# Order and tile offset of the weight parts in a split-float matmul stream: gate, value, q and k units of an encoder block

## The chip, the cores and the metric

The kernel runs on one core of one Trainium2 chip. The metric is the device time of one execution in microseconds, given as the median of several runs. TensorE (PE) does the matrix products, ScalarE (ACT) and VectorE (DVE) do the elementwise work, GpSimd (POOL) and SyncE (SP) issue most of the DMAs. PEld is the loading of stationary weights into PE, which runs beside its matmuls.

## The reference, cut to what matters

The layer is a bidirectional encoder block on 256 tokens of width 2048, all in float32:

```
h = rmsnorm(x);  [q | k | v | u] = h @ w_in
a = rmsnorm(windowed attention with 12 q heads, 4 kv heads)
f = rmsnorm(Fourier mix of u)
x = x + concat(a, f) @ w_out
h = rmsnorm(x);  up = h @ w_up          # w_up: 2048 x 2*5504
gate, value = up[:, :5504], up[:, 5504:]
act = gelu(depthwise_conv3(gate) + b) * value
y = rmsnorm(x + act @ w_down)
```

The products that matter here are the q and k columns of `h @ w_in` (12 + 4 blocks of 128 columns) and the whole of `h @ w_up` (43 blocks of 128 gate columns and 43 of 128 value columns). Each block contracts over 2048 input features.

## The kernel before, in words

**Split floats.** A float32 operand is kept as two parts that PE reads in a faster format (float32r): a high part, which ACT writes as a rounded copy (L168), and a low part, which DVE writes as the remainder (L169). A product is the sum of high times high, high times low and low times high.

**Units.** The work is a sequence of units, each of which has one weight block of 1 MB (128 partitions x 2048 columns) that SP loads into one of three `raw` tiles. `split` (L161) turns it into a `hi` and a `lo` tile; three buffers of each rotate. Each of these tiles has 2176 columns, and `parts_of` (L154) uses 2048 of them, beginning at an offset in columns that the list `shifts` holds for each unit: a pair, one offset for `hi` and one for `lo`. One column is 4 bytes. One buffer lies 2176 columns, 8704 bytes, behind the other.

**The units of the change** are those of q, k, gate and value. In them the weights are the stationary operand. The 2048 columns of `hi` (and of `lo`) are sixteen slices of 128, one for each 128 input features. `still_weights` (L308) adds up, in one bank of PSUM, for each slice one matmul with the high weights that moves 512 columns (256 tokens' high activations and 256 tokens' low ones, L318), and one with the low weights that moves the 256 high ones (L321). So a unit has 16 matmuls of 512 columns and 16 of 256, and each of the 32 loads its own weights. After it, ACT copies one half of the bank and DVE adds the other (`scaled_sum`), for a q or k unit in `qk_out`.

The argument `group` says how many high matmuls stand ahead of as many low ones. With 1 they alternate; with 16 all sixteen high ones come first. The argument `o` says onto which half of the bank the low product is added. Before, these are:

- q and k: group 1; offsets 16 for `hi`, 0 for `lo`.
- gate j: by j modulo 5 group 1, group 1 with the other half, 2, 4 and 16; offsets 16 and 0.
- value j: group 16; the same offset for both tiles, `16 * (j % 8) + 8 * (j // 32)`: 0, 16, 32 ... 112 for j below 32, then 8, 24 ... 120, and 8, 24, 40 for the last three.
- the first gate and the first value unit are a pair: twelve slices of each, then the last four of each, with group 1. Between them come the transposes of the last quarter of the input.

The units of `w_out` and of the late rows of `w_down` have offset 0 in both tiles; those of u and v have 16 in both. There the weights move and the activations stand.

**Order.** It is written out by hand (`ff_items`, L69): sixteen gate and value units in a row; then four groups, each of three gate or value units in a row and after that thirteen times one product of the down-projection and one unit, and one product. A product (`by_parts`, L1046, tiles `ps_P` and `ps_N`) is twelve matmuls of 512 columns. Behind the groups come four late down units, six gate and value units, and the end. While PE works on an item, the split of the item after the next one is made (`ff_step`).

Of the kernel before, what the change touches and what calls it, by code (L numbers as in the profile page):

```python
# [13 lines left out]
P = 128  # L14
D = 2048
S = 256
NK = D // P
# [12 lines left out]
WARM = 7  # L30

U_HEAD, U_ROW = 16, 768


SHIFT = 16

# [32 lines left out]
def ff_items():  # L69


    def ups(tiles):
        return [(kind, j) for j in tiles for kind in ("gate", "val")]

    items = ups(range(8))
    for g in range(N_GROUPS):
        todo = {
            "u": ups(range(8 * g + 8, 8 * g + 16)),
            "s": [("product", g, c, p) for c in range(2) for p in PRODUCTS[c]],
        }  # L80
        items += [todo[c].pop(0) for c in PATTERN]
        assert not any(todo.values())
    items += [("down", 0, c) for c in range(4)] + ups(LAST)
    items += [("down", 1, c) for c in range(4)] + [("last", c) for c in range(4)]
    return items
# [3 lines left out]
def block_kernel(  # L89
# [18 lines left out]
    nc = tc.nc  # L108
# [10 lines left out]
    def bank(pool, name):  # L119
        return pool.tile([P, 512], F32, tag=pool.name, name=name)  # L120
# [1 line left out]

    units = [(w_u_x[i], 2048) for i in range(4)] + [(w_in[i], 2048) for i in range(20)]
    units += [(w_out[i], 2048) for i in range(16)]
    shifts = [(SHIFT, SHIFT)] * 8 + [(SHIFT, 0)] * 16 + [(0, 0)] * 16
    n_front = len(units)
    items, up_index = ff_items(), {}
    for n, it in enumerate(items):
        if it[0] == "product":
            continue  # L130
        up_index[n] = len(units)
        if it[0] in ("gate", "val"):
            units.append((w_up[2 * it[1] + (it[0] == "val")], 2048))
            if it[0] == "gate":
                shifts.append((SHIFT, 0))
            else:
                j = it[1]
                shifts.append((16 * (j % 8) + 8 * (j // 32),) * 2)
            continue
        elif it[0] == "down":  # L140
            units.append((w_down_late[4 * it[1] + it[2]], 2048))
        else:
            units.append((w_down_last[it[1]], 512 * len(LAST)))
        shifts.append((0, 0))
    RAW = 3
    raws, halves = {}, {}
# [7 lines left out]
    def parts_of(i):  # L154
        halves[i] = tuple(
            wp.tile([P, 2176], F32R, tag=h, name=f"{h}{i}", bufs=3)[:, s : s + 2048]
            for h, s in zip(("hi", "lo"), shifts[i])
        )
        return halves[i]
# [87 lines left out]
    ps = bank(dn, "ps_warm")  # L247
# [57 lines left out]
                ps, ah, wl, start=False, stop=last and q == q0 + len(kk) - 1  # L305
            )

    def still_weights(hi, lo, ps, kk, group=1, o=0):  # L308

        for k0 in kk[::group]:
            ks = range(k0, min(k0 + group, kk[-1] + 1))
            for k in ks:
                s = slice(k * P, (k + 1) * P)
                nc.tensor.matmul(ps, hi[:, s], hk(k), start=k == 0, stop=False)  # L318
            for k in ks:
                s = slice(k * P, (k + 1) * P)  # L320
                nc.tensor.matmul(  # L321
                    ps[:, o : o + S], lo[:, s], hk(k)[:, 0:S], start=False, stop=k == NK - 1
                )

    def hk(k):
        return hT[k // 4][:, k % 4, :]
# [18 lines left out]
    def at(when, i, f, *a):  # L345
        when.setdefault(i, []).append((f, a))
# [17 lines left out]
    for k in range(NK):  # L364
        c, q = k // 4, k % 4
        if q == 0:
            hi, lo = (t.rearrange("p (k c) -> p k c", k=4) for t in parts_of(c))
        n = 1 if c < 2 else 2
# [8 lines left out]
        if k < 4:  # L377

            for p, w in enumerate([hi, hi, lo]):
                for b in range(2):  # L380
                    o = p % 2 * S + b * P
                    nc.tensor.matmul(
                        ps_u[b], hk(k)[:, o : o + P], w[:, q, :],
                        start=k == 0 and p == 0, stop=False,
# [348 lines left out]
    for n, (kind, h) in enumerate(QK_ORDER):  # L733

        def work(hi, lo):
            ps = st["ps", kind, h] = bank(mm, f"ps_{kind}{h}")
            still_weights(hi, lo, ps, range(NK))

        unit(N_QK + n, work)
# [50 lines left out]
    for n, (c, kq) in enumerate(OUT_ORDER):  # L790
# [15 lines left out]
        if kq >= 2:  # L806
            part = "a" if kq == 2 else "f"
            ps = ps_a[c] if kq < 3 else ps_a[c, "f"]
# [113 lines left out]
    def ring_load():  # L922
        if ring_next[0] < len(ring):
            key = ring[ring_next[0]]
            ring_next[0] += 1
            ring_tiles[key] = fp.tile([P, 2048], F32, tag="rawd", name="rawd%d%d%s" % key)
            nc.sync.dma_start(ring_tiles[key], weights_of(*key))
# [24 lines left out]
    def first_sums(g, c):  # L952

        a, b = ring_tiles[g, c, "a"], ring_tiles[g, c, "b"]
        x = ring_tiles["x"] = fp.tile([P, 2048], F32, tag="sumw", name=f"sumw{g}{c}", bufs=1)
        nc.vector.tensor_tensor(x, a, b, ALU.add)
        nc.gpsimd.dma_start(b, weights_of(g, c, "d"), accum_op=ALU.add)
# [14 lines left out]
    def ff_step(n):  # L972
        todo, later[:] = list(later), []
        for f in todo:
            next(f, None)
        run(beside, n)
        split_item(n + 2)
        for f in todo:
            for _ in f:
                pass  # L980
        run(behind, n)

    def up_posts(n, kind, j, ps):
        if kind == "gate":
            at(beside, n + 1, scaled_sum, ps, f"g{j}")
            at(beside, n + 2, gate_conv, j)
            at(behind, n + 2, gate_gelu, j)
        else:
            at(beside, n + 1, scaled_sum, ps, f"v{j}")
            at(beside, n + 2, val_mult, j)  # L990
            if j % 8 == 7 and j < 8 * N_GROUPS:
                g = j // 8
                at(behind, n + 1, operand, g, "P1")
                at(behind, n + 2, operand, g, "N4")
                at(behind, n + 3, operand_sums, g, 0)
                at(behind, n + 4, operand, g, "P7")
                at(behind, n + 4, operand, g, "P2")
                at(behind, n + 5, operand_sums, g, 1)
                at(behind, n + 5, operand, g, "N5")
                at(behind, n + 6, operand, g, "N3")  # L1000
                at(behind, n + 7, operand, g, "P6")
            if j >= 8 * N_GROUPS:
                at(behind, n + 2, act_parts, j)
# [42 lines left out]
    def by_parts(ps, o, hi, lo, first, last):  # L1046

        for p in range(4):
            s = slice(p * 512, (p + 1) * 512)
            nc.tensor.matmul(ps, o[:, 0, p, :], hi[:, s], start=first and p == 0, stop=False)  # L1050
            nc.tensor.matmul(ps, o[:, 1, p, :], hi[:, s], start=False, stop=False)  # L1051
            nc.tensor.matmul(ps, o[:, 0, p, :], lo[:, s], start=False, stop=last and p == 3)  # L1052
# [59 lines left out]
    for q in range(2):  # L1112
        kind, j = items[q]
        ps = bank(mm, f"ps_{kind}{j}")
# [6 lines left out]
    for ps, hi, lo in pair:  # L1121
        still_weights(hi, lo, ps, range(12, NK))
# [7 lines left out]
    for n, it in enumerate(items):  # L1130
        if n < 2:
            continue
        if it[0] == "last":
            break
        if n in (8, 9):
            ring_load()
        if n == 13:
            pending.append(lambda: first_sums(0, 0))
        if it[0] in ("gate", "val"):
            kind, j = it  # L1140
            ps = bank(mm, f"ps_{kind}{j}")
            group, o = ((1, 0), (1, S), (2, 0), (4, 0), (16, 0))[j % 5] if kind == "gate" else (16, 0)
            still_weights(*halves.pop(up_index[n]), ps, range(NK), group, o)
            ff_step(n)
            up_posts(n, kind, j, ps)
            continue
        if it[0] == "product":
            kind, g, c, p = it
            end = g == N_GROUPS - 1
            if (c, p) in held:  # L1150
                by_parts(held[c, p], parts[p], *halves.pop(it), g == 0, end)
            else:
                ps = bank(mm, f"ps_{p}{g}{c}")
                by_parts(ps, parts[p], *halves.pop(it), True, True)
                at(beside, n + 1, product_out, g, c, p, ps)
            if end and p == "N4":
                for q in range(3):
                    at(behind, n + 1 + q, shared_out, c, q)
        else:
            kind, g, c = it  # L1160
            hi, lo = halves.pop(up_index[n])
            ps = [bank(mm, f"ps_l{g}{c}{b}") for b in range(2)]
            for b in range(2):
                moving_weights(hi, lo, 512, LATE[g], act.get, b, ps[b], True, True)
            at(beside, n + 1, down_out, c, ps)
            if (g, c) == (0, 0):
                gfb = fp.tile([P, D], F32, tag="sumw", name="gfb", bufs=1)
                nc.gpsimd.dma_start(gfb, normf_g.partition_broadcast(P))
        ff_step(n)
# [153 lines left out]
```

## Time and profile before

| | |
|---|---|
| median of 3 runs | 964.35 us (964.25 to 964.61) |
| the profiled execution | 965.02 us |
| its span | 963.2 us |
| PE busy | 953.3 us, 99% of the span |
| DVE busy | 751.1 us, 78% |
| ACT busy | 534.3 us, 55% |
| granted TensorE clock | 0.998 |
| DMA over the span | 220 GB/s |

The profile names a group of instructions by line, engine and operation, and by the tiles that it writes and reads. The timeline gives each matmul's start and, in the second column, the time from the start of the first of a merged row to the end of its last. Matmuls overlap: a matmul of 512 columns is shown as some 0.39 us long, while the next one starts some 0.23 us behind it. So the time of a unit is read here from the start of its first matmul to the start of the first matmul of what follows it, and the time of one matmul in a run as that difference over their number (its pitch).

### The profile page before, as it was taken

Reading aid. Unit: us, or ns where it says so; the run is one execution under the profiler, and the core shown is the slowest. Engines: PE = TensorE matmul, PEld = TensorE weight load, DVE = VectorE, ACT = ScalarE, POOL = GpSimd, SP = SyncE. Lnnn points to the kernel's source line nnn. Section 1 sums busy time; section 2 is a strip of 40 time slices with the busy share of each in tenths; the row PEclk is TensorE's granted clock in tenths of the full one; section 3 lists DMA queues with packets and bytes.
Section 4 is the critical chain, followed back from the end, with each engine's and each line's share of the span. In section 5 each row is a group of like instructions: output and inputs, shape, how many; then the busy total and the mean of one; then the engine's idle time right before and its main releaser. Section 6 shows DMA issues by size and latency. Waiting matters only on the chain.

```text
span 963.2 us, 12781 instructions
## 1 busy us (share of the span) xinstructions
PE 953.3 (99%) x5085; PEld 819.9 (85%) x5085; DVE 751.1 (78%) x935; ACT 534.3 (55%) x646; POOL 43.4 (5%) x58
## 2 busy tenths in 40 slices
PE   9999999999999999999999999999999999999996
PEld 7888898888888888888888888888888888888885
DVE  7658877576576788787897978988779979887775
ACT  6656666554454446555665555655556655554442
POOL 0000000000000000000000000000000000000003
PEclk9999999999999999999999999999999999999999
DMA  9854444445546676977778786886977687666532
GB/s 369 319 185 150 157 147 159 150 163 212 181 174 242 234 223 193 289 230 254 229 250 243 238 299 218 262 258 207 287 250 240 200 291 217 214 238 219 176 132 88
DMA packets 32108, 211.58 MB, mean 220 GB/s; under 512 B 3504, under 2 KB 4016, under 8 KB 7984
## 3 DMA queue, kind: packets, MB, share of 16 engines
q1 hardware_dynamic: 28448, 184.55, 51.9%
q0 software_dynamic: 3600, 26.22, 14.2%
q8 instruction: 40, 0.66, 0.3%
q14 instruction: 20, 0.16, 0.0%
HBM read 208.65 MB, written 2.10 MB: 219 GB/s over the span
## 4 chain that ended last, share of the span: by engine, by line
PE 98%; DVE 1%; DMA 0%; issue 0%; ACT 0%; POOL 0%; POOLq 0%; DVEq 0%; ACTq 0%
PE ps_val L318 17%; PE ps_gate L318 17%; PE ps_val L321 8%; PE ps_gate L321 8%; PE ps_q L318 5%; PE ps_P L1052 3%; PE ps_P L1051 3%; PE ps_P L1050 3%; PE ps_q L321 2%; PE ps_N L1052 2%; PE ps_N L1050 2%; PE ps_N L1051 2%; PE ps_a L304 2%; PE ps_a L302 2%; PE ps_a L303 2%; PE ps_k L318 2%
## 5 line engine op out<-in xcount | busy, mean ns | idle before, releaser
L169 DVE TENSOR_TENSOR lo<-raw,hi 128x2048 fp32r<-128x2048 f32 (+1 forms) x133 | 302.7, 2276 | 55.2 <-ACT hi L168 55.2
L168 ACT ACTIVATE hi<-raw 128x2048 fp32r<-128x2048 f32 (+1 forms) x133 | 253.4, 1905 | 60.7 <-PE ps_l L303 25.0
L318 PE MATMUL ps_gate<-hU,hi 128*128 128x512 f32 x688 | 212.2, 394 | 0.0
L318 PE MATMUL ps_val<-hU,hi 128*128 128x512 f32 x688 | 168.4, 394 | 0.0
L318 PEld LDWEIGHTS ps_val<-hU,hi 128*128 128x128 f32 x688 | 128.3, 188 | 29.0
L321 PE MATMUL ps_gate<-hU,lo 128*128 128x256 f32 x688 | 145.7, 280 | 0.0
L318 PEld LDWEIGHTS ps_gate<-hU,hi 128*128 128x128 f32 x688 | 122.5, 188 | 21.4
L321 PEld LDWEIGHTS ps_gate<-hU,lo 128*128 128x128 f32 x688 | 117.2, 188 | 10.0
L321 PEld LDWEIGHTS ps_val<-hU,lo 128*128 128x128 f32 x688 | 88.0, 189 | 3.7
L321 PE MATMUL ps_val<-hU,lo 128*128 128x256 f32 x688 | 90.4, 280 | 0.0
L832 ACT ACTIVATE ft_g<-ps_gate 128x256 f32<-128x256 f32 x43 | 16.6, 385 | 127.6 <-PE ps_gate L321 127.6
L832 ACT ACTIVATE ft_v<-ps_val 128x256 f32<-128x256 f32 x43 | 16.5, 384 | 96.9 <-PE ps_val L321 96.9
L318 PE MATMUL ps_q<-hT,hi 128*128 128x512 f32 x192 | 68.1, 398 | 0.0
L321 PE MATMUL ps_q<-hT,lo 128*128 128x256 f32 x192 | 53.6, 279 | 0.0
L1050 PE MATMUL ps_P<-hi_P,op_P 128*128 128x512 f32 x128 | 50.0, 391 | 0.0
L1052 PE MATMUL ps_P<-lo_P,op_P 128*128 128x512 f32 x128 | 50.0, 391 | 0.0
L1051 PE MATMUL ps_P<-hi_P,op_P 128*128 128x512 f32 x128 | 50.0, 391 | 0.0
L942 DVE TENSOR_TENSOR lo_N<-sumw,hi_N 128x2048 fp32r<-128x2048 f32 x16 | 36.6, 2290 | 10.1 <-ACT hi_N L941 10.1
L318 PEld LDWEIGHTS ps_q<-hT,hi 128*128 128x128 f32 x192 | 36.1, 188 | 8.0
L834 DVE TENSOR_TENSOR fa_g<-ps_gate,ft_g 128x256 f32<-128x256 f32 x43 | 18.2, 423 | 28.8 <-ACT ft_g L832 28.8
L302 PE MATMUL ps_a<-hi,cat 128*128 128x512 f32 x96 | 37.9, 394 | 0.0
L1052 PE MATMUL ps_N<-lo_N,op_N 128*128 128x512 f32 x96 | 37.6, 392 | 0.0
(332 smaller groups left out, 1609.1 us busy)
## 6 DMA issues: line engine op xcount, KB each, us to landing
raw<-in_w_up SPq DMA_DIRECT2D x86, 1024.0 KB, 4.9
raw<-in_w_in SPq DMA_DIRECT2D x20, 1024.0 KB, 4.9
raw<-in_w_out SPq DMA_DIRECT2D x16, 1024.0 KB, 4.8
sumw<-in_w_down POOLq DMA_DIRECT2D x16, 1024.0 KB, 8.6
raw<-in_w_down_late SPq DMA_DIRECT2D x8, 1024.0 KB, 4.7
raw<-in_w_down_last SPq DMA_DIRECT2D x4, 768.0 KB, 4.2
ux<-in_w_u_x SPq DMA_DIRECT2D x3, 768.0 KB, 9.7
xs<-in_x SPq DMA_DIRECT2D x4, 512.0 KB, 16.5
```

What stands on the lines that cost most here:

```text
L168: nc.scalar.activation(hi[:, 0:n], raw[:, 0:n], AF.Copy)
L169: nc.vector.tensor_tensor(lo[:, 0:n], raw[:, 0:n], f32(hi[:, 0:n]), ALU.subtract)
L302: nc.tensor.matmul(ps, ah, wh, start=first and q == q0, stop=False)
L303: nc.tensor.matmul(ps, al, wh, start=False, stop=False)
L304: nc.tensor.matmul(ps, ah, wl, start=False, stop=last and q == q0 + len(kk) - 1)
L318: nc.tensor.matmul(ps, hi[:, s], hk(k), start=k == 0, stop=False)
L321: nc.tensor.matmul(ps[:, o : o + S], lo[:, s], hk(k)[:, 0:S], start=False, stop=k == NK - 1)
L832: nc.scalar.activation(tmp, ps[:, S : 2 * S], AF.Copy)
L942: nc.vector.tensor_tensor(lo, src, f32(hi), ALU.subtract)
L1050: nc.tensor.matmul(ps, o[:, 0, p, :], hi[:, s], start=first and p == 0, stop=False)
L1051: nc.tensor.matmul(ps, o[:, 1, p, :], hi[:, s], start=False, stop=False)
L1052: nc.tensor.matmul(ps, o[:, 0, p, :], lo[:, s], start=False, stop=last and p == 3)
```

## The change

All q, k, gate and value units get one form: sixteen matmuls with the high weights, then sixteen with the low ones, with the low product on the first half of the bank, and both weight tiles without an offset. The pair at the beginning of the up-projection gets twelve and twelve, then four and four. The number of matmuls, what they multiply, the order of the units and the instruction lists of the other engines stay as they are.

```diff
-    shifts = [(SHIFT, SHIFT)] * 8 + [(SHIFT, 0)] * 16 + [(0, 0)] * 16
+    shifts = [(SHIFT, SHIFT)] * 8 + [(0, 0)] * 32
...
             units.append((w_up[2 * it[1] + (it[0] == "val")], 2048))
-            if it[0] == "gate":
-                shifts.append((SHIFT, 0))
-            else:
-                j = it[1]
-                shifts.append((16 * (j % 8) + 8 * (j // 32),) * 2)
+            shifts.append((0, 0))
...
-    def still_weights(hi, lo, ps, kk, group=1, o=0):
-        for k0 in kk[::group]:
-            ks = range(k0, min(k0 + group, kk[-1] + 1))
-            for k in ks:
-                s = slice(k * P, (k + 1) * P)
-                nc.tensor.matmul(ps, hi[:, s], hk(k), start=k == 0, stop=False)
-            for k in ks:
-                s = slice(k * P, (k + 1) * P)
-                nc.tensor.matmul(
-                    ps[:, o : o + S], lo[:, s], hk(k)[:, 0:S], start=False, stop=k == NK - 1
-                )
+    def still_weights(hi, lo, ps, kk):
+        for k in kk:
+            s = slice(k * P, (k + 1) * P)
+            nc.tensor.matmul(ps, hi[:, s], hk(k), start=k == 0, stop=False)
+        for k in kk:
+            s = slice(k * P, (k + 1) * P)
+            nc.tensor.matmul(
+                ps[:, 0:S], lo[:, s], hk(k)[:, 0:S], start=False, stop=k == NK - 1
+            )
...
-            group, o = ((1, 0), (1, S), (2, 0), (4, 0), (16, 0))[j % 5] if kind == "gate" else (16, 0)
-            still_weights(*halves.pop(up_index[n]), ps, range(NK), group, o)
+            still_weights(*halves.pop(up_index[n]), ps, range(NK))
```

## The prediction

> **What bounds the kernel now.** I read the page's busy times and chain first, then the busy times of the middle of the span, then PE's timeline unit by unit.
>
> ```profile
> PE 953.3 (99%) x5085; PEld 819.9 (85%) x5085; DVE 751.1 (78%) x935; ACT 534.3 (55%) x646; POOL 43.4 (5%) x58
> PE 98%; DVE 1%; DMA 0%; issue 0%; ACT 0%; POOL 0%; POOLq 0%; DVEq 0%; ACTq 0%
> L318 PE MATMUL ps_gate<-hU,hi 128*128 128x512 f32 x688 | 212.2, 394 | 0.0
> L321 PE MATMUL ps_val<-hU,lo 128*128 128x256 f32 x688 | 90.4, 280 | 0.0
> ```
>
> PE is the whole chain, and its groups show no idle time ahead of them (the last column). A nanosecond less per matmul is a nanosecond less of the kernel, as long as PE stays supplied. The densest stretch says how far the next engine is:
>
> ```profile
> core 0: us, PE busy (x) PEld busy (x) DVE busy (x) ACT busy (x) POOL busy (x), PEclk, DMA share, GB/s
> 360.00:870.00 510.00, 510.00 (x2704) 437.45 (x2703) 431.64 (x449) 291.89 (x284) 20.69 (x24) 1.00 0.77 243
> ```
>
> DVE has 78 us of 510 free there, against the 5 us or so that PE can lose in it.
>
> The timeline then prices the change, because the value units already have the new order, with many offsets. These are, in order, value 8 (offset 0), value 14 (offset 96), value 16 (0), value 20 (64), gate 24 (16 for high, 0 for low, new order) and value 24 (0):
>
> ```profile
> 355.15 3.84 PE L318 MATMUL ps_val<-hU,hi 128*128 128x512 f32 x16
> 358.83 2.05 PE L321 MATMUL ps_val<-hU,lo 128*128 128x256 f32 x16
> 360.71 3.83 PE L318 MATMUL ps_gate<-hU,hi 128*128 128x512 f32 x16
> ...
> 452.31 3.90 PE L318 MATMUL ps_val<-hU,hi 128*128 128x512 f32 x16
> 456.05 2.05 PE L321 MATMUL ps_val<-hU,lo 128*128 128x256 f32 x16
> 457.94 0.40 PE L1050 MATMUL ps_P<-hi_P,op_P 128*128 128x512 f32 x1
> ...
> 482.97 3.84 PE L318 MATMUL ps_val<-hU,hi 128*128 128x512 f32 x16
> 486.65 1.98 PE L321 MATMUL ps_val<-hU,lo 128*128 128x256 f32 x16
> 488.46 0.62 PE L318 MATMUL ps_gate<-hU,hi 128*128 128x512 f32 x2
> ...
> 546.85 3.84 PE L318 MATMUL ps_val<-hU,hi 128*128 128x512 f32 x16
> 550.53 1.98 PE L321 MATMUL ps_val<-hU,lo 128*128 128x256 f32 x16
> 552.34 0.39 PE L1050 MATMUL ps_P<-hi_P,op_P 128*128 128x512 f32 x1
> ...
> 605.17 3.83 PE L318 MATMUL ps_gate<-hU,hi 128*128 128x512 f32 x16
> 608.84 2.04 PE L321 MATMUL ps_gate<-hU,lo 128*128 128x256 f32 x16
> 610.72 3.84 PE L318 MATMUL ps_val<-hU,hi 128*128 128x512 f32 x16
> 614.40 1.98 PE L321 MATMUL ps_val<-hU,lo 128*128 128x256 f32 x16
> 616.21 0.40 PE L318 MATMUL ps_gate<-hU,hi 128*128 128x512 f32 x1
> ```
>
> Subtract starts: value 14 takes 457.94 - 452.31 = 5.63 us, value 16, 20 and 24 take 5.49 each. The 32 matmuls are the same; the pitch is not: value 14 has 234 ns per high and 118 per low matmul, value 16 has 230 and 113. Value 8 has no offset either and takes 5.56: its high pitch is 230, its low pitch 118. So a unit settles into one of a few repeating patterns, and the offset, together with what ran just before, chooses it.
>
> **The change, part by part.** From the timeline I took every unit's time in this way. The 84 gate and value units outside the first pair, in mean us:
>
> - gates, 42: alternating 5.586 (8 units), alternating onto the other half 5.607 (9), twos 5.550 (9), fours 5.631 (8), sixteens 5.551 (8): together 234.56 us.
> - values, 42, by offset modulo 64 columns: 0: 5.502 (7), 16: 5.578 (8), 32: 5.618 (8), 48: 5.614 (8), 8: 5.607 (3), 24: 5.614 (3), 40: 5.629 (3), 56: 5.642 (2): together 234.83 us.
>
> The sum is 469.38 us, 5.588 a unit. Offsets 64 apart (256 bytes) give the same: 16 and 80 both 5.58, 0 and 64 both 5.49 to 5.50. Buffers lie 34 times 256 bytes apart, so all three should be alike; values at offset 16 modulo 64 took 5.58 in both that they used.
>
> *The new form in the gate and value units.* Seven units had it already, at offset 0 or 64: value 12, 20 and 28, each behind a product, 5.495; value 4, 16 and 24, each behind a gate, 5.490; value 8, behind a gate in fours, 5.558. After the change 55 of the 84 stand behind a product and one behind a late down unit (twelve-matmul and 24-matmul runs of the same 512-column kind): 56 x 5.495 = 307.72 us. One (gate 1) follows four small matmuls, which now makes its first pitch 0.315 us where others have 0.23, and keeps that: 5.575. The other 27 follow a unit of the new form directly, which no row shows. Bounds: 5.490 (value 16, behind a low matmul of offset 0 with a 112 ns pitch) and 5.558 (value 8, behind one with a 122 ns pitch). A low run at offset 0 ends with 113 ns, so value 16 is the nearest row: 27 x 5.490 = 148.23. Together 461.52, a gain of **7.86 us** (6.0 at the other bound).
>
> *The first pair.* Its pieces take 4.21 + 4.32 + 1.40 + 1.41 = 11.34 us (258.94 to 271.07, less the transposes between). At 230 and 113 ns per matmul, with the slow first pitch of value 0 (0.317) kept, they take 11.06, at 118 ns for the low ones 11.20. Gain 0.14 to 0.28; I take **0.2**, since nothing says which pattern runs of twelve and four reach.
>
> *The q and k units.* They take 67.52 + 22.34 = 89.86 us. Nine follow score matmuls, seven follow small ones and have a first pitch of 0.316 to 0.320. All in the good pattern they take 16 x 5.49 + 7 x 0.085 = 88.44, a gain of 1.42; all in value 8's pattern 16 x 0.07 = 1.12 more, a gain of 0.30. Their old order fell into several patterns (5.55 for two units, 5.61 for seven behind scores), so I take the middle, **0.85**.
>
> *Products behind the units.* They take 2.746 us in the mean, and 2.75 behind value 12 (424.54 to 427.29). Nothing, at most 0.2.
>
> *Supply, costed at nothing.* The high tile of a unit is ready 4.96 us or more ahead of its first matmul; the low tile, at the worst (gate 34), 1.0 us ahead of the unit, and the first low matmul now comes 3.7 us after the unit's start instead of 0.23. The high buffer comes free some 1.8 us earlier, the low one at the same place. No wait is added, and no queue of SP, POOL, ACT or DVE is changed. Without that cover, a late low tile would stop PE for what is missing, in each of the 52 units of the groups that alternate with products.
>
> The sum is 7.86 + 0.2 + 0.85 = 8.9 us off the profiled execution's 965.02 us, which gives 956.1. That execution stood 0.67 us over the median of the runs, so against the median 964.35 the forecast is **955.4 us**, 0.9% less.
>
> **The rivals.**
>
> *Direct followers settle as value 8 did.* 27 units at 5.558 cost 27 x 0.068 = 1.8 us: 957.2. For it speaks that it happened once in four; against it, that value 8's forerunner ended in a pattern which no unit has any more.
>
> *All settle so.* Then 56 units cost 0.063 more and 27 cost 0.068 more, q and k 0.55: 955.4 + 5.4 + 0.55 = 961.4. Value 12, 20 and 28 speak against it: three of three behind products were good, to the nanosecond.
>
> *Offset and order do nothing*, and neighbours make the differences. The change then moves only equal matmuls about: 964.35. Against it: value 12, 20, 28 (offset 64) and value 14, 22, 30 (offset 96) have the same order and follow the same kind of product, and take 5.495 and 5.631. The Trainium skill, "TensorE: Matmul & The Clock Gate", Part 2, states this rival as a rule: PE has two independent read ports, and loading the next weights takes no read bandwidth from the running matmul. By that rule the sum would be zero; those six rows disagree with it.
>
> *The other side: all lock into the worst pattern.* Offset 32 shows that an offset alone does not decide: value 6 took 5.55, value 14 took 5.63. If a stream of only new units drove itself into high 234 and low 118, the 84 units would take 473.0 (3.6 more), q and k 90.7 (0.8 more), the pair nothing: 968.8. It decides from a mean unit of 5.607 on, where 100 units have lost 1.9 us. For it speaks only that the third buffer with offset 0 and the direct sequence are not in the trace; against it, none of seven units passed 5.56.
>
> **How the numbers follow.** My forecast has a chance of 0.70, the direct followers' rival 0.14, the "all" rival 0.07, no effect 0.03, the worst pattern 0.04; 0.02 are left for something else that helps. The lowest sum is all gains at their best: 7.86 + 0.28 + 1.42 + 0.2 = 9.8, 954.6; I set 954.3. The upper end takes in the second case with q and k at their worst: 957.2 + 0.6 = 957.8, and some of the mixed cases toward the third: 958.5. A measurement of this kernel can tell some 0.2% (1.9 us) from no change. All cases but two are faster by more: 0.93 faster, 0.03 the same, 0.04 slower.
>
> **What would show it.** In the timeline of the changed kernel each gate and value unit behind a product takes 5.49 to 5.50 us, with 16 low matmuls over 1.98 us, and each direct follower the same. If direct followers show 2.05 us for the low run, the first rival is right; if the units behind products do as well, the second. The granted clock, the products' 2.75 us and the absence of idle time ahead of PE should stay. The prediction is wrong at its root if units at offset 0 take 5.6 us, or if PE waits for a low tile.

## The result, and the profile after

| | before, run beside it | after |
|---|---|---|
| median | 964.3 us (964.22 to 964.61, 4 runs) | 956.1 us (955.9 to 956.45, 4 runs) |
| ratio | | 0.9915 (95% interval 0.9898 to 0.9932) |
| profiled execution | 965.02 us, span 963.2 | 956.12 us, span 954.4 |
| granted clock | 0.998 | 0.997 |

The change makes the kernel 8.2 us faster. The page of the kernel after, with its busy times, its chain and three of its groups (the last column is the idle time ahead of the group):

```profile
PE 944.7 (99%) x5085; PEld 814.4 (85%) x5085; DVE 750.7 (79%) x935; ACT 534.2 (56%) x646; POOL 43.3 (5%) x58
...
PE 98%; DVE 1%; DMA 0%; issue 0%; ACT 0%; POOL 0%; POOLq 0%; DVEq 0%; ACTq 0%
...
L310 PE MATMUL ps_gate<-hU,hi 128*128 128x512 f32 x688 | 165.5, 392 | 0.0
L310 PE MATMUL ps_val<-hU,hi 128*128 128x512 f32 x688 | 165.2, 392 | 0.0
...
L313 PE MATMUL ps_val<-hU,lo 128*128 128x256 f32 x688 | 86.2, 277 | 0.0
```

PE is still the whole chain, nothing waits ahead of its groups, and its busy time fell by 8.6 us, the span by 8.8. The groups must be read with care: the gates' high matmuls show 165.5 us of busy time where they showed 212.2, but that is no gain of 47 us. Where sixteen high matmuls stand in a row they overlap each other, and the overlap is counted once in the group; where they alternated, each overlapped a low matmul of another group. The mean of one is 392 ns against 394. Only starts tell what was gained.

The cover held. In the densest stretch (the busy time of each engine from 360 to 870 us) DVE still has 72 of 510 us free:

```profile
core 0: us, PE busy (x) PEld busy (x) DVE busy (x) ACT busy (x) POOL busy (x), PEclk, DMA share, GB/s
360.00:870.00 510.00, 510.00 (x2726) 437.87 (x2725) 437.59 (x453) 293.15 (x285) 20.64 (x24) 1.00 0.78 245
```

PE's timeline of the kernel after has three kinds of gate and value unit. First value 1, gate 2 and value 2, each straight behind another unit, then gate 10, behind a product, with the product behind it (start, then length of the merged row):

```profile
275.35 3.82 PE L310 MATMUL ps_val<-hU,hi 128*128 128x512 f32 x16
279.00 2.05 PE L313 MATMUL ps_val<-hU,lo 128*128 128x256 f32 x16
280.89 3.84 PE L310 MATMUL ps_gate<-hU,hi 128*128 128x512 f32 x16
284.56 1.98 PE L313 MATMUL ps_gate<-hU,lo 128*128 128x256 f32 x16
286.38 3.82 PE L310 MATMUL ps_val<-hU,hi 128*128 128x512 f32 x16
...
374.60 3.84 PE L310 MATMUL ps_gate<-hU,hi 128*128 128x512 f32 x16
378.28 1.98 PE L313 MATMUL ps_gate<-hU,lo 128*128 128x256 f32 x16
380.09 0.39 PE L1042 MATMUL ps_N<-hi_N,op_N 128*128 128x512 f32 x1
```

Value 1 takes 280.89 - 275.35 = 5.54 us, gate 2 5.49, gate 10 5.49 (5.495 from the starts in ns). Over the whole trace the kinds are exact:

| units | count | predicted, us each | measured |
|---|---|---|---|
| behind a product or down unit | 56 | 5.495 | 5.495, all |
| gate 1, behind small matmuls | 1 | 5.575 | 5.573 |
| gate behind a value | 13 | 5.490 | 5.490, all |
| value behind a gate | 14 | 5.490 | 5.543 to 5.544, all |
| together | 84 | 461.52 | 462.27 |

The value behind a gate is the one kind that came out otherwise. From the starts in ns, its sixteen high matmuls take 3.66 us and its sixteen low ones 1.88 (118 ns each), where a gate behind a value shows 3.68 and 1.81 (113 ns).

### The profile page after: what moved, and what is told of

Same layout as the page of the kernel before. It is cut to its first block, busy times and chain, and to the rows that moved or that the text cites. A ratio compares the mean times of both kernels' runs of the same rounds, so it can differ in the third digit from the quotient of the medians.

```text
span 954.4 us, 12779 instructions
## 1 busy us (share of the span) xinstructions
PE 944.7 (99%) x5085; PEld 814.4 (85%) x5085; DVE 750.7 (79%) x935; ACT 534.2 (56%) x646; POOL 43.3 (5%) x58
## 4 chain that ended last, share of the span: by engine, by line
PE 98%; DVE 1%; DMA 0%; issue 0%; ACT 0%; POOL 0%; POOLq 0%; DVEq 0%; ACTq 0%
PE ps_gate L310 17%; PE ps_val L310 17%; PE ps_val L313 8%; PE ps_gate L313 8%; PE ps_q L310 5%; PE ps_P L1042 3%; PE ps_P L1043 3%; PE ps_P L1044 3%; PE ps_q L313 2%; PE ps_N L1042 2%; PE ps_N L1043 2%; PE ps_a L299 2%; PE ps_a L297 2%; PE ps_a L298 2%; PE ps_N L1044 2%; PE ps_k L310 2%
## 5 line engine op out<-in xcount | busy, mean ns | idle before, releaser
L310 PE MATMUL ps_gate<-hU,hi 128*128 128x512 f32 x688 | 165.5, 392 | 0.0
L310 PE MATMUL ps_val<-hU,hi 128*128 128x512 f32 x688 | 165.2, 392 | 0.0
L310 PEld LDWEIGHTS ps_gate<-hU,hi 128*128 128x128 f32 x688 | 128.1, 188 | 27.6
L313 PEld LDWEIGHTS ps_val<-hU,lo 128*128 128x128 f32 x688 | 85.4, 188 | 3.7
L313 PEld LDWEIGHTS ps_gate<-hU,lo 128*128 128x128 f32 x688 | 84.6, 188 | 3.8
L313 PE MATMUL ps_val<-hU,lo 128*128 128x256 f32 x688 | 86.2, 277 | 0.0
L313 PE MATMUL ps_gate<-hU,lo 128*128 128x256 f32 x688 | 85.2, 276 | 0.0
L310 PE MATMUL ps_q<-hT,hi 128*128 128x512 f32 x192 | 46.5, 394 | 0.0
L1043 PE MATMUL ps_N<-hi_N,op_N 128*128 128x512 f32 x96 | 37.6, 392 | 0.0
L1042 PE MATMUL ps_N<-hi_N,op_N 128*128 128x512 f32 x96 | 37.6, 392 | 0.0
```

Of the source, the lines that this page charges most:

```text
L313: nc.tensor.matmul(ps[:, 0:S], lo[:, s], hk(k)[:, 0:S], start=False, stop=k == NK - 1)
```

## The experiments

All kernels here do the same matmuls on the same numbers; only the order and the place of operands differ. Times of units are differences of starts in the timeline. A "high run" is a unit's sixteen high matmuls, a "low run" its sixteen low ones.

**1 and 2. Each half of the change alone.** `order_only` is the kernel after with the offsets of before; `offsets_only` is the kernel before with offset 0 in all q, k, gate and value tiles.

```diff
  # order_only, against the kernel after
-    shifts = [(SHIFT, SHIFT)] * 8 + [(0, 0)] * 32
+    shifts = [(SHIFT, SHIFT)] * 8 + [(SHIFT, 0)] * 16 + [(0, 0)] * 16
...
-            shifts.append((0, 0))
+            if it[0] == "gate":
+                shifts.append((SHIFT, 0))
+            else:
+                j = it[1]
+                shifts.append((16 * (j % 8) + 8 * (j // 32),) * 2)
  # offsets_only, against the kernel before: the reverse of these lines
```

> All units with the sixteen high matmuls first, but the tiles keep the offsets that they had. Theory (the offset chooses the pattern, the order alone does little): gates at offsets 16/0 take 5.55 us behind products and 5.53 to 5.56 behind values, as the eight gates in sixteens did, 1.3 us less in all; values stay at 234.8 us within 0.5; q and k gain some 0.4, the pair 0.1. Together 1.8 us off 964.3: 962.5. Rival (the order makes the gain): 956 to 957. Rival (the parts add, each a half): 960.

> All q, k, gate and value tiles without offset, but gates keep their five orders, and q and k alternate. Theory: values fall from 234.8 to some 231.2 us (5.495 behind products, 5.49 to 5.56 behind gates). Alternating units get worse, not better: the first value unit of the kernel before alternated at offset 0 and took 0.353 us a pair, 5.64 a unit, against 5.60. So 17 alternating gates lose 0.8, sixteens gain 0.4, q and k lose 0.5, twos and fours unknown: 961.5, between 960 and 963. Rival (the zero offset makes the gain whatever the order): 956 to 957.

| | median, us | ratio to before | gate and value units | q and k units |
|---|---|---|---|---|
| before | 964.37 | | 469.38 | 89.86 |
| order only | 962.3 (10 runs) | 0.9977 (0.9968 to 0.9987) | 467.85 | 89.30 |
| offsets only | 960.68 (4 runs) | 0.9961 (0.9946 to 0.9976) | 465.16 | 90.60 |
| both (after) | 956.1 | 0.9915 (0.9898 to 0.9932) | 462.27 | 88.98 |

Alone the order brings 2.1 us and the offset 3.7, in sum 5.8; together they bring 8.2 to 8.3. So both are causes, and some 2.5 us of the gain needs both. The unit times bear that out: the gate and value units gain 1.53 and 4.22 us by the halves and 7.11 by both, the q and k units 0.56 and -0.74, and 0.88 by both, so 1.36 and 1.06 us come only with the two together. The order alone came out as expected (962.5). The offsets alone lie in their range, but not by the expected terms: the 17 alternating gates lost 0.2 us in sum and not 0.8, and the fours, whose change had been left open, gained 0.7. The gates show why the parts do not add. With the new order at offsets 16 and 0 every gate behind a product takes 5.552 to 5.553 us, here gate 10 of `order_only` (381.02 - 375.47):

```profile
375.47 3.83 PE L314 MATMUL ps_gate<-hU,hi 128*128 128x512 f32 x16
379.14 2.05 PE L317 MATMUL ps_gate<-hU,lo 128*128 128x256 f32 x16
381.02 0.39 PE L1046 MATMUL ps_N<-hi_N,op_N 128*128 128x512 f32 x1
```

With offset 0 and the old orders they take 5.588 (alternating, 12 units, where they took 5.599), 5.554 (twos, 5.548 before), 5.538 (fours, 5.633 before) and 5.495 (sixteens, 5.552 before). Offset 0 is thus not good in itself: it made twos no faster, the four alternating gates behind values slower (5.65 to 5.66 us where they took 5.55 to 5.62), and the q and k units, which alternate, 0.74 us slower in sum. It is good where sixteen high matmuls stand in a row. The values had that order already. Behind a product they go to 5.495 whatever they took before, in all 28. This is value 21 of `offsets_only` (567.66 - 562.17 = 5.49), whose offset was 80 and whose time was 5.58:

```profile
562.17 3.84 PE L314 MATMUL ps_val<-hU,hi 128*128 128x512 f32 x16
565.85 1.98 PE L317 MATMUL ps_val<-hU,lo 128*128 128x256 f32 x16
567.66 0.39 PE L1046 MATMUL ps_P<-hi_P,op_P 128*128 128x512 f32 x1
```

**3. The new order at another common offset.** If being all alike is what helps, any common offset should do.

```diff
-            shifts.append((0, 0))
+            shifts.append((32, 32))     # and the q and k units likewise
```

> The changed kernel with offset 32 instead of 0 in both tiles of every q, k, gate and value unit: as uniform as the change, and the same order. Theory (the value of the offset counts): 56 units behind products take 5.631, those behind units 5.55 to 5.63, q and k lose 1.7 us and the pair 0.15: 956.1 + 11.5 = 967.6, between 965 and 968.5, slower than the kernel before. Rival (what helped is that neighbouring units are alike): 956 to 957.

Measured: 965.12 us (10 runs), ratio 1.0008 (0.9998 to 1.0018): all of the gain is gone. Being alike is worth nothing by itself. Behind a product a unit takes 5.626 to 5.631 us (value 9: 373.44 - 367.81), as before at offset 32 or 96; straight behind another it takes 5.546 to 5.557 (value 1: 281.86 - 276.31), better than the 5.6 that I had reckoned with. The q and k units lost 0.8 us where I had expected 1.7, and the products gained 0.46 (153.26 us against 153.72). These three make 965.1 out of 967.6.

```profile
276.31 3.89 PE L310 MATMUL ps_val<-hU,hi 128*128 128x512 f32 x16
280.04 1.98 PE L313 MATMUL ps_val<-hU,lo 128*128 128x256 f32 x16
281.86 3.89 PE L310 MATMUL ps_gate<-hU,hi 128*128 128x512 f32 x16
...
367.81 3.90 PE L310 MATMUL ps_val<-hU,hi 128*128 128x512 f32 x16
371.55 2.05 PE L313 MATMUL ps_val<-hU,lo 128*128 128x256 f32 x16
373.44 0.40 PE L1042 MATMUL ps_P<-hi_P,op_P 128*128 128x512 f32 x1
```

At offset 32 the rows look alike for the 3.9 us of high matmuls, and the low run takes one of the two lengths, 1.98 or 2.05. So two things are to be explained: what the place does, and what picks the length of the low run.

**4. A map of both offsets.** The 55 units behind products get 55 pairs of offsets, in steps of 8 columns; all other units stay at 0.

```diff
-            shifts.append((0, 0))
+            m = sum(items[q - 1][0] == "product" for q in range(1, n) if items[q][0] in ("gate", "val"))
+            shifts.append((8 * (m // 8 % 8), 8 * (m % 8)) if items[n - 1][0] == "product" else (0, 0))
```

> The changed kernel, but the 55 gate and value units behind products take in turn each pair of offsets from 0, 8 ... 56 for the high tile and 0, 8 ... 56 for the low one (up to 48/48); all other units 0/0. A table of what each pair costs. Theory (each load of weights meets the reading of the moving operand, so each tile's own offset counts): the high run's time depends on the high offset alone, 3.68 us for 0, 3.67 for 16, 3.74 for 32; the low run's on the low offset and on how the high run ended: 1.81 for low offset 0 after high offset 0, 1.88 after 16. Rival (only the difference of the two offsets counts): 8/8, 16/16 and so on take 5.495 as 0/0 does. Some pair may be below 5.49; the floor, with no matmul delayed, is 16 x (226.7 + 113.3) = 5.44 us. In all some 959 to 963 us.

One execution, 962.62 us. The time of sixteen high matmuls goes by the high tile's offset alone, whatever the low tile's:

| offset of the high tile | 0 | 8 | 16 | 24 | 32 | 40 | 48 |
|---|---|---|---|---|---|---|---|
| high run, us | 3.681 to 3.688 | 3.729 to 3.736 | 3.668 to 3.679 | 3.724 to 3.731 | 3.739 to 3.745 | 3.732 to 3.738 | 3.715 to 3.721 |

The low run takes 1.813 us only at 0 and 0, 1.825 to 1.829 at low offset 32 behind a high one of 0, 8, 24 or 48, and 1.864 to 1.927 elsewhere. Pairs of equal offsets differ (0 and 0: 5.495; 16 and 16: 5.582; 32 and 32: 5.631), so the distance between the two weight tiles does not decide it: that rival falls. Of the 55 pairs 0 and 0 is the best.

**5 and 6. Whose place is it?** The offset may matter by the weight tile's own place, or by its place against the moving operand that PE reads at the same time. `moving16` leaves the weights at 0 and lays the moving operand `hT` 16 columns further; `both16` moves both. The weight buffers become 2112 columns wide to make room, still a multiple of 64.

```diff
+    def moving_tile(c, name):
+        t = base.tile([P, 2112], F32R, tag=f"hT{c}", name=name)
+        return t[:, 16:2064].rearrange("p (k c) -> p k c", k=4)
...
-        t = base.tile([P, 4, 512], F32R, tag=f"hT{c}", name=f"hU{c}")
+        t = moving_tile(c, f"hU{c}")
...
  # both16 only
-            shifts.append((0, 0))
+            shifts.append((16, 16))     # and the q and k units likewise
```

> The changed kernel, but the four tiles of activations that these matmuls move (hT) begin 16 columns, 64 bytes, later; the weight tiles stay at offset 0 (their buffers are 2112 columns apart instead of 2176, to make room, still a multiple of 64). Theory (a load of weights meets the reading of the moving operand, so what counts is where one lies against the other): the same as weights moved back by 16, which is 48/48 in the table: units behind products take 5.611 instead of 5.495, with high runs of 3.715 and low ones of 1.896; the kernel 963 to 967 us. Rival (what counts is the weight tile's own place): 5.495 and 956 us.

> As the last, with the weight tiles 16 columns later too. Theory (place against place): back to 5.495 behind products, 5.49 and 5.543 behind units, 956 us. Rival (the weight tile's own place): 5.582 as 16/16 in the table, some 962 us.

`moving16` took 969.53 us in one execution, and no unit keeps 5.49 though every weight tile still begins at a multiple of 256 bytes from where it was: 5.627 behind products, 5.612 to 5.635 straight behind units. Value 9 of `moving16` (376.50 - 370.88; its low run goes at 119 ns):

```profile
370.88 3.89 PE L310 MATMUL ps_val<-hU,hi 128*128 128x512 f32 x16
374.60 2.06 PE L313 MATMUL ps_val<-hU,lo 128*128 128x256 f32 x16
376.50 0.40 PE L1046 MATMUL ps_P<-hi_P,op_P 128*128 128x512 f32 x1
```

The weight tile's own place, the rival that gave 956, falls. The row is the one that the map had at a distance of -16 (48 and 48: 5.611), near to 5.627 but not equal. The time missed the range I had set by 2.5 us. Against the kernel after, the gate and value units lost 10.3 us, q and k 1.5, the products 0.4, and the u and v units, which read the same `hT`, 1.1. Of the last, at least 0.32 us comes from the move: the first 48 matmuls of v take 10.88 us in every run without it and 11.20 in `moving16` and `both16`. The u units take 22.2 to 23.2 us in the runs that leave them alone, so the rest can be chance.

`both16` took 961.12 us in one execution. Value 1, gate 2 (straight behind units) and value 9 (behind a product):

```profile
276.31 3.84 PE L310 MATMUL ps_val<-hU,hi 128*128 128x512 f32 x16
279.99 1.98 PE L313 MATMUL ps_val<-hU,lo 128*128 128x256 f32 x16
281.80 3.82 PE L310 MATMUL ps_gate<-hU,hi 128*128 128x512 f32 x16
285.46 2.04 PE L313 MATMUL ps_gate<-hU,lo 128*128 128x256 f32 x16
287.35 3.84 PE L310 MATMUL ps_val<-hU,hi 128*128 128x512 f32 x16
...
367.35 3.83 PE L310 MATMUL ps_val<-hU,hi 128*128 128x512 f32 x16
371.01 2.05 PE L313 MATMUL ps_val<-hU,lo 128*128 128x256 f32 x16
372.89 0.40 PE L1046 MATMUL ps_P<-hi_P,op_P 128*128 128x512 f32 x1
```

Straight behind units the two values of the kernel after are back, 5.49 and 5.54, with gates and values in exchanged roles. Behind products it is 5.548, neither the 5.495 of my theory nor the 5.582 of the rival: the theory of 956 missed by 56 x 0.053 = 3.0 us there; the products, which follow another pattern, lost 1.2 us and the u and v units 0.85. So straight behind units the place against the moving operand decides. Behind products it does not decide alone: there a run begins in another way (under 7), behind a product whose own operands had not been moved. No run has the narrower weight buffers without a move, so whether their width has a part in the 5.548 is not shown. The Trainium skill, "SBUF — State Buffer", section "Who interferes with whom", gives PE two independent read ports and says that it never waits on anyone; here the same 32 matmuls behind the same product take 5.495, 5.627 or 5.548 us with only addresses changed, so the two operands' places act on the time all the same. Whether one read waits for the other, or what else inside the chip makes the difference, no run here shows.

**7. What picks the low run.** The single starts of the kernel after show a cycle of three pitches, 226, 229 and 232 ns, in every high run at offset 0. These are the sixteen high pitches and the first two low ones (ns, worked out from the starts in the trace), with a unit of `both16` in the last line:

```
gate 10  236 235 232 232 226 229 231 226 229 232 226 229 232 226 229 231 | 114 113
gate 2   233 236 229 232 225 230 231 226 229 232 226 229 232 225 230 231 | 114 113
value 1  226 229 232 226 229 232 225 230 231 226 229 232 226 229 232 225 | 118 118
value 9  229 230 231 227 228 232 226 230 230 226 229 233 225 230 231 226 | 117 119   (both16, behind a product)
```

Gate 2 is in the cycle from its third pitch on, gate 10 from its fourth, and both end on 231; value 1 follows a low run at 113 ns, is in the cycle at once, and sixteen being five threes and one it ends on 225. Of the 84 units, 70 end on 231 or 232 and go on at 113 ns, and 14 end on 225 or 226 and go on at 118. `both16` keeps to the same split: its 70 units that end on 225 to 227 go on at 118 ns, its 14 that end on 231 to 233 at 113. There the runs behind products are in the cycle almost at once, end on 225 to 227 and have the slower low run, and so take 5.548. If the last high pitch sets the low run, then a first stretch of 15, 12 or 9 slices instead of 16 brings the low run behind it to 113 ns. The run `map_fine` tried first stretches of many lengths on values behind gates and, besides, finer offsets, in steps of 2 and 4 columns, behind products.

```diff
...
+RUNS = {1: 15, 2: 12, 3: 9, 4: 13, 5: 14, 6: 6, 7: 3, 8: 8, 16: 1, 24: 2, 32: 4, 40: 15, 41: 7, 42: 10}
...
-            still_weights(*halves.pop(up_index[n]), ps, range(NK))
+            hi, lo = halves.pop(up_index[n])
+            first = RUNS.get(j, NK) if kind == "val" else NK
+            still_weights(hi, lo, ps, range(first))
+            if first < NK:
+                still_weights(hi, lo, ps, range(first, NK))
```

> Two questions in one execution. First, units behind products take offsets that are not multiples of 8 (steps of 2 and 4 columns); is any pair below 5.49? Theory: a high run at offset 4 or 12 lies between its neighbours 0 (3.682 us), 8 (3.733) and 16 (3.668), so no unit is below 5.48. Second, 14 value units behind a gate take a first stretch of n high and n low matmuls, then the rest (n is 15, 12, 9, 13, 14, 6, 3, 8, 1, 2, 4, 15, 7, 10). Theory: behind a good low run the high matmuls repeat 226, 229, 232 ns from the first on, and a low run goes at 113 ns only if the last high matmul before it took 232, that is where n is a multiple of three; sixteen end on 226, and the low run goes at 118. So n = 15, 12, 9, 6, 3 have a first low run at 113 to 114 ns, the others at 117 to 118; with n = 15 the unit takes some 5.48 us instead of 5.543. Rival (a low run's pitch does not depend on where the high run stops): all at 118, and units longer than 5.543 for the second stretch. The kernel 957 to 962 us.

One execution, 961.1 us. Value 1 with 15 and 1 (281.10 - 275.63 = 5.47; 5.476 in ns):

```profile
275.63 3.60 PE L314 MATMUL ps_val<-hU,hi 128*128 128x512 f32 x15
279.06 1.86 PE L317 MATMUL ps_val<-hU,lo 128*128 128x256 f32 x15
280.76 0.39 PE L314 MATMUL ps_val<-hU,hi 128*128 128x512 f32 x1
280.99 0.28 PE L317 MATMUL ps_val<-hU,lo 128*128 128x256 f32 x1
281.10 3.84 PE L314 MATMUL ps_gate<-hU,hi 128*128 128x512 f32 x16
```

First stretches of 15 give 5.476 (twice), of 12 5.490, of 9 5.503; of 13, 14, 10 and 7 5.540 to 5.556. The others (8, 6, 4, 3, 2 and 1 slices: 5.568, 5.531, 5.506, 5.517, 5.540, 5.492) did not begin with the cycle's pitch of 225 or 226 ns, but with 228 to 235, so their lengths test nothing; 6 and 3, for which 113 ns had been expected, have 117 to 121. By stretches, the second ones included, the rule is sharper than by units: of the 28 stretches of these fourteen values, 10 end on a high pitch of 231 to 233, and all have their low matmuls at 113 to 114 ns in the mean; 17 end on 225 to 230, and all have them at 116 to 119; one, a single matmul of 235 ns, has 118.

The finer offsets showed a second pattern: at a high offset of 20 the sixteen high matmuls take 3.626 us behind a product, 226.7 ns each with no slow one among them, but the low run behind them goes at 118, and the unit takes 5.51 to 5.52. No pair of offsets in this map was under 5.50. One expectation failed: the high run at offset 12 was to lie between those at 8 and 16 (3.73 and 3.67 us) and took 3.66.

**8. Can the high run of 3.63 us have a low run of 1.81 behind it?** By the rule of experiment 7 a delay in the last high matmul should do it. All units get high offset 20; behind products either the low offset varies, or the sixteenth high slice alone is laid elsewhere.

```diff
+            m = sum(items[q - 1][0] == "product" for q in range(1, n) if items[q][0] in ("gate", "val"))
+            low, tail = ENDS[m] if items[n - 1][0] == "product" else (0, None)
+            shifts.append((20, low))
+            if tail is not None:
+                last_at[len(units) - 1] = 1984 + tail
```

> All q, k, gate and value units have offset 20 in the high tile, whose high runs took 3.625 us behind products, 226.7 ns a matmul, the floor seen; at low offset 0 the low run then took 1.885. Here the 55 units behind products vary in how the low run is met: 29 even low offsets, and 26 units in which the sixteenth high slice alone lies at another place (0, 4 ... 60 modulo 64, in a copy of its own). Theory (the low run's pitch is set by where its first load of weights falls against the reading that goes on): all high runs 3.63 us, and for some of these ends the low run takes 1.81, the unit 5.44 to 5.46 us. Rival (a low run at 113 ns needs a delay in the high run before it, as it had each time so far): no low run below 1.86, no unit below 5.50, except where the moved slice itself is delayed by some 5 ns, and those take 5.45. The kernel 956 to 960 us.

One execution, 961.79 us. With the sixteenth slice at 18 or 40 columns modulo 64 and low offset 0, the last two high pitches are 228 and 232, the low run goes at 113, and the unit takes 5.447 us. Those two fit the rule. Nine other places of the slice (2, 4, 10, 14, 24, 28, 44, 48 and 56) do not: their last high pitch is 231 to 236 as well, and the low run goes at 118 (5.52 to 5.54 us). And low offset 38 needed no delay: behind a last pitch of 226 its low run fell from 121 to 113 ns within five matmuls, and the unit took 5.460. Low offset 32 with the slice at 0, 8, 24 or 48 gave 5.454 to 5.467. So at high offset 20 a late last matmul is not enough, and at low offset 38 it is not needed: the rule is one of offset 0, and what singles out 18 and 40 stays open. Away from the products offset 20 is bad: 5.52 to 5.62 us straight behind units, most of them over 5.61, and q and k lost 1.2 us against the kernel after.

**9 and 10. The best cases of the maps put to use.** `best` takes the kernel after, gives the 56 units behind products and down units high offset 20 with the sixteenth slice at 18 modulo 64 (which costs ACT and DVE one more instruction per unit), and splits the values behind gates into 15 slices and 1. `simple` uses offsets 20 and 38 behind products instead, without the moved slice.

```diff
  # best
+            if n and items[n - 1][0] not in ("gate", "val"):
+                shifts.append((20, 0))
+                last_at[len(units) - 1] = 1984 + 18
+            else:
+                shifts.append((0, 0))
...
  # both
+            first = NK - (kind == "val" and items[n - 1][0] == "gate")
...
  # simple
+            shifts.append((20, 38) if n and items[n - 1][0] not in ("gate", "val") else (0, 0))
```

> The changed kernel with two things from the tables. The 56 units behind a product or a late down unit have offset 20 for the high tile and 0 for the low one, with the sixteenth high slice apart, at 18 modulo 64: 5.447 instead of 5.495, 2.7 us. The 14 value units behind a gate take fifteen high and fifteen low matmuls, then the last of each: 5.476 instead of 5.543, 0.9 us. Theory (the pattern and where the run stops): 956.1 - 3.6 = 952.5, between 952 and 953.2. Rival (DVE's and ACT's second instruction for the slice apart, in 56 units, makes PE wait, or the patterns of the tables hold only beside their neighbours there): 954 to 957.

> As the last, but the 56 units have offsets 20 and 38 and no slice apart, so no instruction is added: 5.460 in the table, 2.0 us less than the change, and 0.9 from the value units: 956.1 - 2.9 = 953.2, between 952.7 and 954. The four units that follow such a unit directly meet a low tile at 38, which no run has shown: within 0.3 us.

| | median, us (4 runs each) | ratio to before | gate and value units |
|---|---|---|---|
| best | 952.81 (952.7 to 953.11) | 0.988 (0.9865 to 0.9895) | 458.62 |
| simple | 953.93 (953.69 to 954.13) | 0.989 (0.9874 to 0.9907) | 459.38 |

Value 9 of `best` (371.42 - 365.97 = 5.45):

```profile
365.97 3.80 PE L319 MATMUL ps_val<-hU,hi 128*128 128x512 f32 x16
369.61 1.98 PE L322 MATMUL ps_val<-hU,lo 128*128 128x256 f32 x16
371.42 0.39 PE L1051 MATMUL ps_P<-hi_P,op_P 128*128 128x512 f32 x1
```

In `best` all 56 units behind products and down units take 5.446 or 5.447 us, all 14 values behind gates 5.476 or 5.477, and the gates behind them 5.490 again. Against the kernel after that is 56 x 0.0485 + 14 x 0.067 = 3.65 us of gate and value time, and 3.3 us in the median; the products, which now follow another pattern, gave back 0.46 us (154.18 against 153.72). The median lies inside the expected range of 952 to 953.2. `simple` has 5.460 in place of 5.447 and lost 0.75 us of unit time by it; its median lies 0.7 above the value expected, inside the range.

## Why the prediction was right, point by point, and the term that was not

The forecast was 955.4 us, the median is 956.1. Term by term:

| term | predicted, us | measured |
|---|---|---|
| gate and value units | 7.86 | 469.38 - 462.27 = 7.11 |
| first pair | 0.2 | 11.34 - 11.21 = 0.13 |
| q and k units | 0.85 | 89.86 - 88.98 = 0.88 |
| products | 0, at most 0.2 | 153.78 - 153.72 = 0.06 |
| sum | 8.9 | 8.2 |

- **Units behind products.** The three rows of value 12, 20 and 28 carried over to the nanosecond, to all 28 gates and 28 values. The rival that all settle as value 8 did is out, and so is the worst pattern, which no gate or value unit of the kernel after met.
- **Direct followers: the term that was mis-sized.** Of the two bounds for 27 units, 5.490 and 5.558, I took the lower one for all, since value 16, behind a low run at 112 ns, seemed the nearest row to a unit behind a low run at 113. Thirteen gates took 5.490. Fourteen values took 5.543, which is 14 x 0.053 = 0.74 us and the whole miss. The reason that I gave was the wrong way round: the gates that took 5.490 stand behind values whose low runs go at 118 ns, and the values that took 5.543 stand behind gates at 113. A value behind a gate at 113 is in the cycle at once and ends on 225 or 226; a gate behind a value at 118 enters it at its third pitch and ends on 231 or 232. So it was luck that 5.490 came out for half of these units. The loss is less than half of what the first rival gave (1.8 us), and by the opposite path: it was not the gate ahead ending badly but the gate ahead ending well that slowed the value. The single pitches of the trace of before held a part of the answer: value 4 and 24, behind gates whose low runs go at 117 to 119, enter the cycle at the third pitch, end on 231 or 232 and take 5.490; value 8 enters it later, ends on 229 and has 118 behind it. What a unit of the new form does straight behind another at 113 ns, no row of before showed.
- **Both parts act.** The rival that offset and order do nothing is refuted from both sides: each change alone is faster by an interval that leaves out 1, and the same order at offset 32 is back at the time of before.
- **The pair** took 4.18 + 4.26 + 1.38 + 1.39 us. Its low runs of twelve go at 118 ns, the upper of the two patterns I had bounded it by, so its gain is just below the lower bound of 0.14.
- **q and k.** Behind scores nine units take 5.475 to 5.558 us, seven of them in the good pattern; the seven behind small matmuls keep a slow first pitch (0.313 to 0.319) and 118 ns low runs, 5.63 to 5.65. So the middle that I took was right as a sum of good and bad, not because each was middling. One of each kind in the kernel after, q7 behind small matmuls, 126.38 - 120.75 = 5.63, and q8 behind scores, 133.72 - 128.25 = 5.47:

```profile
120.75 3.91 PE L310 MATMUL ps_q<-hT,hi 128*128 128x512 f32 x16
124.50 2.05 PE L313 MATMUL ps_q<-hT,lo 128*128 128x256 f32 x16
126.38 0.40 PE L688 MATMUL ps_o<-pt,v_hi 128*128 128x256 f32 x2
...
128.25 3.82 PE L310 MATMUL ps_q<-hT,hi 128*128 128x512 f32 x16
131.91 1.98 PE L313 MATMUL ps_q<-hT,lo 128*128 128x256 f32 x16
133.72 0.40 PE L688 MATMUL ps_o<-pt,v_hi 128*128 128x256 f32 x2
```

- **Supply at nothing.** PE shows no idle time ahead of any group of the units, and the clock stayed. The later first use of the low tile and the earlier release of the high one moved nothing that can be seen in the time.

The terms give 8.2 us, as the medians do. The two profiled executions differ by 8.9; of the 0.7 between, 0.36 lies in the u and v units, which the change does not touch and which vary from 44.5 to 45.1 us over the runs that leave them alone.

## What to carry to other kernels

Where PE is the whole chain, a list of matmul starts by unit is worth more than any busy time: the same 32 matmuls behind a product took from 5.447 to 5.659 us here, 4%, by the places of the operands alone. Offsets of the weights 64 columns (256 bytes) apart did the same, and where the moving operand lies counts as well. Look at single pitches in such a run, not only at its sum: at offset 0 they repeat with a period of three, and a run whose length leaves the wrong remainder, or which starts at another step, hands the next run a slower pattern. Such an effect is local to operands, order and neighbours, so it has to be measured for each kernel: offset 0 was the best pair of the first map behind products (5.495) and was beaten there by 20 and 38 (5.460), was no help for gates in twos, and was worse for the alternating q and k units.

## What the runs showed of the hardware that was not expected

- The pitch of a 512-column float32r matmul with its own weights is not one number: high runs went at a steady 226.7 ns (high offset 20), in the cycle 226, 229, 232 (offset 0, mean 229), or at 234 in the mean (offset 32), and the 256-column one at 113.3 or some 118, at a granted clock of 0.997 to 0.998 throughout.
- At offset 0 the last high pitch foretells the low run: 231 ns or more within the cycle and it goes at 113, 230 or less and it goes at 118, for all 84 units of the kernel after and, with both operands moved by 16, all 84 of `both16`. At high offset 20 it does not hold. Why, and what the three steps are, stays open.
- What runs ahead of a product changes its time, by no rule that these runs show: the 56 products took 153.26 us at offset 32, 153.72 in the kernel after, 154.18 in `best` and 154.89 in `both16`.
